# Moving the eviction and the store of the per-layer embedding's units to other engines

## The chip, the cores and the metric

The kernel runs on one core of one Trainium2 chip. The metric is device microseconds of one execution, as the median of several runs; lower is better.

## The reference: what is computed

One layer of a streaming encoder on 1024 prompt tokens and 8 samples of 16 new tokens, each sample with 1024 cached frames, in float32.

```python
xn = rms_norm(x, norm_g)
u, g_pool, c_q, c_kv, k_r, g_mla = jnp.split(xn @ w_in, SPLIT_IDX, axis=-1)
pool_out = multiscale_pool(...) * silu(g_pool)
attn = chunk_causal_attention(q_nope, q_rope, k_nope, krope_all, v, q_pos, k_pos)
h = x + concat([pool_out, attn * silu(g_mla)]) @ w_out
gate = sigmoid(rms_norm(h, ple_norm_g) @ w_ple_gate + b_ple_gate)
y = h + gate * (p @ w_ple)
```

The change is about the product `p @ w_ple` of the last line: `p` has 256 columns for each of the 1152 tokens, and `w_ple` is 256 x 2048. It hangs on nothing else, so it can be computed at any time before the last stage.

## The kernel before

Arrays lie transposed: 128 channels on the partitions, tokens along the free axis, in NT = 3 blocks of TB = 384 tokens. Every matrix product is made of three matmuls (`mm3`, lines 77 to 79): each operand is split into a rounded high half and a low half, and high x high, low x high and high x low are summed. A split (`split`, lines 68 and 69) is a copy by ScalarE, which makes the high half, and a subtraction, by VectorE or GpSimd, which makes the low one. So what TensorE multiplies has always passed ScalarE and then one of the others.

The stages follow one another: input projections and the pooling branch (to about 805 us of the profile), key and query projections of the attention (`phase2`, to about 985 us), attention of the samples over their caches (`attend_samples`, to about 1297 us), attention of the prompt (`attend_prompt`, to about 1670 us), output projection and gate (`phase5`).

The class `Embed` makes `p @ w_ple`. `block(t, cts)` handles one token block: it loads the two row tiles of `p` (line 782, tensor `pT`) and splits them into `h` and `l`, and then makes sixteen units, one for each group `ct` of 128 output channels. A unit loads its weights (`wraw`, line 786, 128 KB, ScalarE's DMA queue), splits them into `wh` and `wl` (two buffers each), makes six matmuls into one PSUM bank (`p`, one buffer; in the last block two units of three use a bank `k` of the sample attention instead), evicts the bank into a tile `ev` (line 794) and stores it to the scratch `ple` in device memory (line 795, 192 KB). The last stage reads `ple` again, more than 600 us later.

The 48 units are filler. Block 0 and half of block 1 are traced beside `phase2`, the other half of block 1 in the first sample (`between`), block 2 in the last weighing of the samples (`fill` in `attend_samples`; there, `issue_after(sh.last.ins)` holds its matmuls behind the last matmul of the sample scores). Behind them come the value projection of the samples (`ph`, `wvh`, lines 1429 to 1446) and the scores `s` of head 0 of the prompt attention, in whose gaps matmuls `f` of the output projection run (`out_units`, lines 1093 to 1121; weights `wraw` from `w_out`, moving tiles `M0h`, `M0l` from `mixp`). The prompt's heads are loaded by `load` (lines 1144 to 1166): tiles `qh`, `kh`, `stk`, `vh`, whose low halves GpSimd makes.

The order on each engine is not written out by hand. The tile framework schedules the traced instructions with a timing model of its own, and each engine then executes its list strictly in order, waiting where an input or a buffer is not there. A DMA is issued in order too, by the engine on whose queue it stands, and an engine that waits to issue one executes nothing behind it. So an edit of one line can move instructions anywhere.

Of the kernel before, what the change touches and what calls it, by code (L numbers as in the profile page):

```python
# [8 lines left out]
AF = mybir.ActivationFunctionType  # L9
# [10 lines left out]
P = 128  # L20
KT = D // P
TB = 384
# [742 lines left out]
class Embed:  # L765
# [8 lines left out]
    def block(self, t, cts=range(KT), bank=None):  # L774
        k, nc, io, pl = self.k, self.k.nc, self.k.io, self.pl
        if t != self.at:
            self.at = t
            self.ph = k.t(pl, [P, 2, TB], "h", F32R)
            self.pl_ = k.t(pl, [P, 2, TB], "l", F32R)
            for c in range(2):  # L780
                raw = k.t(pl, [P, TB], "raw")
                nc.scalar.dma_start(raw[:], io["pT"][t][:, c, :])
                k.split(self.ph[:, c, :], self.pl_[:, c, :], raw[:])
        for ct in cts:
            raw = k.t(pl, [P, 2, P], "wraw", bufs=4)
            nc.scalar.dma_start(raw[:], io["w_ple"][ct])
            wh = k.t(pl, [P, 2, P], "wh", F32R, bufs=self.bufs)
            wl = k.t(pl, [P, 2, P], "wl", F32R, bufs=self.bufs)
            k.split(wh[:], wl[:], raw[:])
            ps = bank() if bank and ct % 3 else k.t(self.pp, [P, 512], "p", bufs=self.banks)  # L790
            for c in range(2):
                k.mm3(ps[:, :TB], wh[:, c, :], wl[:, c, :], self.ph[:, c, :], self.pl_[:, c, :], c == 0, c == 1)
            ev = k.t(pl, [P, TB], "ev", bufs=2)
            nc.vector.tensor_copy(ev[:], ps[:, :TB])
            nc.scalar.dma_start(self.sc["ple"][t][:, ct, :], ev[:])


class Shared:
# [652 lines left out]
def phase5(k, sc, wp):  # L1451
# [16 lines left out]
    def fill(b, c, src):  # L1468
        raw = ev()
        nc.sync.dma_start(raw[:], src)  # L1470
        k.split(b[0][:, c, :], b[1][:, c, :], raw[:])

    mix = [block(mp, t, "M", KT // 2) for t in range(NT)]
    for t in range(NT):
        for c in range(KT // 2):
            fill(mix[t], c, sc["mixm"][t][:, c, :])
    yield
    pp = es.enter_context(tc.tile_pool(name="p6p", bufs=1, space=PSUM, reuse_waits="tile"))
    ap = es.enter_context(tc.tile_pool(name="p6a", bufs=1, side="right", reuse_waits="tile"))
    res = [block(ap, t, "A", KT) for t in range(NT - 1)]  # L1480
    acc = [k.t(ep, [P, TB], f"R{t}") for t in range(NT)]
    half = range(KT // 2, KT)
# [28 lines left out]
    w = w_gate(0)  # L1511
    lp = es.enter_context(tc.tile_pool(name="p6l", bufs=1, reuse_waits="tile"))
    res.append(block(lp, NT - 1, "A", KT))
    for c in range(KT):
        fill(res[-1], c, sc["h"][:, c, :])
# [164 lines left out]
```

## Time and profile before

| | us |
|---|---|
| median of 3 runs | 2307.72 |
| lowest and highest | 2302.0, 2310.47 |
| the profiled execution | 2295.69 |
| its span, first to last instruction | 2293.9 |
| TensorE busy in it | 2217.6 |
| VectorE, ScalarE, GpSimd busy | 1450.2, 985.4, 345.7 |

The profile speaks of engines as PE (TensorE; PEld is its weight load), DVE (VectorE), ACT (ScalarE), POOL (GpSimd) and SP (SyncE, which only issues DMAs). A q behind the name (ACTq) is the engine's sequencer. In rows of the timeline, the first two numbers are the start and the duration in us, then come engine, line and operation, output <- input, and in brackets how long the engine had been idle and what ended the wait. In rows of waits stand the total in us, how often, and the longest. In rows of groups stand the count, busy us and mean ns, and the idle time ahead.

### The profile page before, as it was taken

The numbers are of one execution on the slowest core, as the hardware profiler recorded it, in microseconds if no ns is written. First come the engines' busy times: TensorE is split into PE (matmuls) and PEld (weight loads), VectorE is DVE, ScalarE is ACT, GpSimd is POOL, SyncE is SP. The second block draws the span as 40 slices with busy tenths as digits, with TensorE's granted clock in tenths as the row PEclk, the third lists the DMA queues.
The fourth block names the chain that finished last, engine by engine and source line by source line (L and its number), as shares of the span: only waits on it lengthen the run. The fifth ranks groups of instructions, "written<-read, shape, count | busy, mean of one in ns | idle before, by whom it ended". The sixth has DMA issues, their size and how long they took to land.

```text
span 2293.9 us, 35989 instructions
## 1 busy us (share of the span) xinstructions
PE 2217.6 (97%) x12856; PEld 2160.4 (94%) x12856; DVE 1450.2 (63%) x3056; ACT 985.4 (43%) x2181; POOL 345.7 (15%) x317
## 2 busy tenths in 40 slices
PE   8989999999899999989999899999999999999999
PEld 7989999999899989979998799999999999999998
DVE  6787777776777668868887765555553345344343
ACT  6533335443333466756665543343342233232222
POOL 0000000001111000033552532221002221111110
PEclk9999999999999999999999799999999999999999
DMA  9574336556666766482222844443263333223221
GB/s 297 185 245 156 126 122 217 166 164 178 184 186 186 220 201 189 122 252 95 92 71 73 246 152 153 129 154 124 82 198 112 101 120 110 86 92 98 85 87 64
DMA packets 257299, 339.24 MB, mean 148 GB/s; under 512 B 45024, under 2 KB 207200, under 8 KB 257120
## 3 DMA queue, kind: packets, MB, share of 16 engines
q1 hardware_dynamic: 234240, 304.18, 42.9%
q10 hardware_dynamic: 19296, 23.21, 3.1%
q0 software_dynamic: 3584, 9.56, 1.7%
q8 instruction: 101, 1.65, 0.3%
q14 instruction: 78, 0.64, 0.1%
HBM read 235.74 MB, written 101.12 MB: 147 GB/s over the span
## 4 chain that ended last, share of the span: by engine, by line
PE 54%; DMA 7%; DVE 6%; issue 2%; ACT 2%; POOL 1%; SPq 0%; ACTq 0%; DVEq 0%; POOLq 0%
PE mm L77 8%; PE mm L79 8%; PE mm L78 8%; PE f L77 3%; PE f L79 3%; PE f L78 3%; PE k L78 2%; PE k L79 2%; PE k L77 2%; PE t L1213 1%; DMA rawcq<-cq 1%; PE o L79 1%; PE o L78 1%; PE s L78 1%; PE s L79 1%
## 5 line engine op out<-in xcount | busy, mean ns | idle before, releaser
L68 ACT ACTIVATE wh<-wraw 128x1024 fp32r<-128x1024 f32 (+3 forms) x237 | 182.2, 770 | 212.9 <-PE mm L177 125.7
L69 DVE TENSOR_TENSOR wl<-wraw,wh 128x1024 fp32r<-128x1024 f32 (+3 forms) x235 | 210.6, 897 | 69.9 <-ACT wh L68 67.3
L1536 DVE TENSOR_TENSOR ev<-mm,R 128x384 f32<-128x384 f32 x48 | 26.7, 557 | 174.2 <-PE mm L79 170.3
L1537 ACT ACTIVATE ev<-ev,gains 128x384 f32<-128x384 f32 x48 | 29.4, 612 | 224.5 <-DVE ev L1536 124.5
L71 ACT ACTIVATE wh<-wraw,gains 128x128 fp32r<-128x128 f32 x256 | 82.0, 391 | 52.5 <-ACT wh L71 31.6
L704 POOL DMA_DIRECT2D u<-u x24 | 13.1, 544 | 602.1 <-DVE frs3a L88 509.3
L1214 ACT ACTIVATE pth<-t 128x512 fp32r<-128x512 f32 (+2 forms) x96 | 46.3, 486 | 131.8 <-PE t L1213 130.8
L72 DVE SCALAR_TENSOR_TENSOR wl<-wraw,gains,wh 128x128 fp32r<-128x128 f32 x256 | 88.0, 390 | 17.5 <-ACT wh L71 16.4
L77 PE MATMUL k<-wkh,ch 128*128 128x448 f32 x256 | 95.2, 373 | 2.1 <-ACT ch L68 1.3
L78 PE MATMUL k<-wkh,cl 128*128 128x448 f32 x256 | 93.6, 365 | 0.6 <-DVE cl L69 0.6
L79 PE MATMUL k<-wkl,ch 128*128 128x448 f32 x256 | 93.7, 366 | 0.0
L79 PE MATMUL mm<-A2l,wh 128*128 128x384 f32 x256 | 86.0, 336 | 0.0
L77 PE MATMUL mm<-A2h,wh 128*128 128x384 f32 x256 | 86.0, 336 | 0.0
L78 PE MATMUL mm<-A2h,wl 128*128 128x384 f32 x256 | 86.0, 336 | 0.0
L77 PE MATMUL mm<-A0h,wh 128*128 128x384 f32 x256 | 85.8, 335 | 0.0
L79 PE MATMUL mm<-A0l,wh 128*128 128x384 f32 x256 | 85.7, 335 | 0.0
L78 PE MATMUL mm<-A1h,wl 128*128 128x384 f32 x256 | 85.7, 335 | 0.0
L78 PE MATMUL mm<-A0h,wl 128*128 128x384 f32 x256 | 85.7, 335 | 0.0
L79 PE MATMUL mm<-A1l,wh 128*128 128x384 f32 x256 | 85.5, 334 | 0.0
L77 PE MATMUL mm<-A1h,wh 128*128 128x384 f32 x256 | 85.5, 334 | 0.0
L1498 DVE TENSOR_TENSOR ev<-mm,ev 128x384 f32<-128x384 f32 x48 | 26.8, 558 | 86.3 <-PE mm L79 85.9
L1342 ACT ACTIVATE sq<-k 128x896 f32<-128x896 f32 x64 | 58.5, 914 | 51.7 <-PE k L1339 50.0
(803 smaller groups left out, 7822.6 us busy)
## 6 DMA issues: line engine op xcount, KB each, us to landing
wraw<-w_in SPq DMA_DIRECT2D x89, 512.0 KB, 4.6
part<-o SPq DMA_DIRECT2D x93, 192.0 KB, 2.7
q<-part SPq DMA_DIRECT2D x93, 192.0 KB, 3.4
wraw<-w_out SPq DMA_DIRECT2D x64, 256.0 KB, 3.4
wraw<-w_ple_gate SPq DMA_DIRECT2D x64, 256.0 KB, 3.2
ple<-ev ACTq DMA_DIRECT2D x48, 192.0 KB, 3.0
fev<-xT SPq DMA_DIRECT2D x48, 192.0 KB, 2.4
hp<-fev SPq DMA_DIRECT2D x48, 192.0 KB, 1.9
```

The source lines that it names most:

```text
L68: nc.scalar.activation(hi, src, AF.Copy)
L69: eng.tensor_tensor(lo, src, hi, ALU.subtract)
L71: nc.scalar.activation(hi, src, AF.Copy, scale=scale)
L72: eng.scalar_tensor_tensor(lo, src, scale, hi, ALU.mult, ALU.subtract)
L77: mm(out, sh, mh, start=start, stop=False)
L78: mm(out, sl, mh, start=False, stop=False)
L79: self.last = mm(out, sh, ml, start=False, stop=stop)
L1214: nc.scalar.activation(pth[:, :n, qq], tp[:, :n, :], AF.Copy)
L1342: nc.scalar.activation(sq[:].rearrange("p (g c) -> p g c", g=2), ps[:, :2, :KW], AF.Square)
L1498: nc.vector.tensor_tensor(h[:], ps[:, :TB], h[:], ALU.add)
L1536: nc.vector.tensor_tensor(g[:], ps[:, :TB], R[t][:], ALU.mult)
L1537: nc.scalar.activation(g[:], g[:], AF.Sigmoid, bias=k.b_ple_gate[:, ct:ct + 1])
```

## The change: what it does

```diff
@@ Embed.block
             for c in range(2):
-                raw = k.t(pl, [P, TB], "raw")
+                raw = k.t(pl, [P, TB], "ev", bufs=3)
                 nc.scalar.dma_start(raw[:], io["pT"][t][:, c, :])
                 k.split(self.ph[:, c, :], self.pl_[:, c, :], raw[:])
...
-            ev = k.t(pl, [P, TB], "ev", bufs=2)
-            nc.vector.tensor_copy(ev[:], ps[:, :TB])
-            nc.scalar.dma_start(self.sc["ple"][t][:, ct, :], ev[:])
+            ev = k.t(pl, [P, TB], "ev", bufs=3)
+            nc.scalar.activation(ev[:], ps[:, :TB], AF.Copy)
+            nc.gpsimd.dma_start(self.sc["ple"][t][:, ct, :], ev[:])
```

The eviction of a unit is made by ScalarE instead of VectorE. The store is issued from GpSimd's queue instead of ScalarE's. The raw tile of `p`, which had one buffer of its own, and the two buffers of `ev` become three buffers that both use. The room in on-chip memory stays the same. The scheduler then orders all engines anew: the first difference lies where block 0 begins, the last one in the last head of the prompt attention; what comes after is in the same order.

On ScalarE, at the beginning of block 2 (`ev` and `ple` are of the units, `wh_13701` is the weight of the second unit, `wh_13733` of the fourth, `wh_13749` of the fifth; `qh`, `kh` belong to head 0 of the prompt), before:

```order
L68 ACTIVATE wh_13701<-wraw_13699 128x256
L68 ACTIVATE wh_13717<-wraw_13715 128x256
L795 DMA ple_24_83<-ev_13680 128x384
L786 DMA wraw_13763<-w_ple 128x256
L795 DMA ple_24_83<-ev_13696 128x384
L68 ACTIVATE wh_13733<-wraw_13731 128x256
L786 DMA wraw_13779<-w_ple 128x256
L795 DMA ple_24_83<-ev_13712 128x384
L68 ACTIVATE wh_13749<-wraw_13747 128x256
```

and now:

```order
L794 ACTIVATE ev_13680<-p_13673 128x384
L68 ACTIVATE wh_13701<-wraw_13699 128x256
L794 ACTIVATE ev_13696<-k_13689 128x384
L68 ACTIVATE wh_13717<-wraw_13715 128x256
L786 DMA wraw_13763<-w_ple 128x256
L786 DMA wraw_13779<-w_ple 128x256
L794 ACTIVATE ev_13712<-k_13705 128x384
L68 ACTIVATE wh_13733<-wraw_13731 128x256
L68 ACTIVATE wh_13749<-wraw_13747 128x256
L794 ACTIVATE ev_13728<-p_13721 128x384
```

The stores have left the list. The evictions stand in it, and the cast of the fourth unit's weights now stands behind the eviction of the third, with the fifth's beside it.

On SyncE's queue, behind the loads for the prompt's heads (`qT`, `kT`, `qrT`, `v`) at the end of block 2 (`w_out` is for the output projection, `mixm` is the result of the value projection), before:

```order
L1151 DMA raw_14367<-v_102 128x512
L110 DMA wraw_14240<-w_out 128x512
L110 DMA wraw_14246<-w_out 128x512
L110 DMA wraw_14252<-w_out 128x512
L1151 DMA raw_14700<-qT_103 128x512
L1446 DMA mixm_18_77<-gate_13923 128x2x128
L1151 DMA raw_14706<-kT_101 128x512
L1161 DMA raw_14712<-qrT_104 64x512 x2
L110 DMA wraw_14258<-w_out 128x512
```

and now:

```order
L1151 DMA raw_14367<-v_102 128x512
L1446 DMA mixm_18_77<-gate_13923 128x2x128
L1151 DMA raw_14700<-qT_103 128x512
L1151 DMA raw_14706<-kT_101 128x512
L1446 DMA mixm_18_77<-gate_13923 128x2x128 x2
L1161 DMA raw_14712<-qrT_104 64x512 x2
L1151 DMA raw_14718<-v_102 128x512
L1446 DMA mixm_18_77<-gate_13923 128x2x128
L1177 DMA gate_14064<-gm_10_69 128x384
```

The loads of `w_out` come later: behind all four stores of the value projection and, further down, behind the first six loads of `mixp`. Their casts on ScalarE and their subtractions on VectorE moved with them, behind those of the value projection.

On TensorE, in head 0 of the prompt attention (`s` are scores of one block of queries, `t` the transposes of the softmax of an earlier block, `f` the output projection), before:

```order
L1213 MATMUL t_14159<-ident_134,e_14139 128x128 x2
L77 MATMUL f_14264<-M0h_14058,wh_14242 128x384
L78 MATMUL f_14264<-M0h_14058,wl_14243 128x384
L77 MATMUL s_14300<-kh_13560,qh_14101 128x512
L78 MATMUL s_14300<-kh_13560,ql_14102 128x512
L79 MATMUL s_14300<-kl_13561,qh_14101 128x512
```

and now:

```order
L1213 MATMUL t_14293<-ident_134,e_14220 128x128 x4
L77 MATMUL f_14264<-M0h_14058,wh_14242 128x384
L77 MATMUL s_14493<-kh_13560,qh_14101 128x512
L78 MATMUL s_14493<-kh_13560,ql_14102 128x512
L79 MATMUL s_14493<-kl_13561,qh_14101 128x512
```

The first `f` stood ahead of the fifth block's scores (`s_14300`); it now stands ahead of the seventh's (`s_14493`). On GpSimd, which had only the low halves in this place, the sixteen stores stand between them: four ahead of head 0's `ql` and `kl`, two behind these, and so on, one or two at a time.

## The prediction

> **What bounds the kernel now.** I read the page's first part, then a table of stages, and only then who waited for whom inside the stages in which units of `Embed` run.
>
> ```profile
> PE 2217.6 (97%) x12856; PEld 2160.4 (94%) x12856; DVE 1450.2 (63%) x3056; ACT 985.4 (43%) x2181; POOL 345.7 (15%) x317
> ```
>
> TensorE is busy for 97% of the 2293.9 us span, and the change adds and removes no matmul. So an edit on the other engines can be worth only what it puts into or takes out of TensorE's 76 us of idle time, and the time in which TensorE runs at a reduced clock. The table says where these are. Its columns are the stretch, its length, busy time of PE, PEld, DVE, ACT and POOL, the granted clock, the DMA share and GB/s.
>
> ```profile
> 800.00:985.00 185.00, 177.32 (x995) 164.81 (x994) 141.75 (x439) 129.23 (x446) 1.96 (x8) 0.97 0.57 172
> 985.00:1005.00 20.00, 13.03 (x67) 10.14 (x66) 16.45 (x44) 8.09 (x17) 0.44 (x1) 1.00 0.91 273
> 1005.00:1245.00 240.00, 238.52 (x1448) 225.95 (x1448) 199.19 (x372) 160.61 (x366) 112.12 (x68) 1.00 0.31 99
> 1245.00:1285.00 40.00, 30.86 (x156) 26.79 (x154) 27.95 (x65) 17.78 (x40) 17.86 (x15) 0.87 0.68 202
> 1285.00:1310.00 25.00, 20.78 (x95) 18.32 (x94) 14.71 (x38) 13.13 (x33) 7.86 (x7) 0.66 0.83 255
> 1310.00:1700.00 390.00, 386.24 (x2435) 372.79 (x2434) 228.04 (x483) 161.24 (x343) 75.76 (x61) 1.00 0.46 144
> ```
>
> I take length minus busy time times clock as what a stage loses. 985 to 1005 us loses 7.0 us. 1245 to 1310 us loses 40 - 30.86 x 0.87 = 13.2 and 25 - 20.78 x 0.66 = 11.3, together 24.5 us, of which 13.4 are idle and the rest half clock. 1005 to 1245 and 1310 to 1700 lose 1.5 and 3.8 us: there TensorE is full, and moving work between the others gives nothing. So the change is worth at most 7.0 + 24.5 = 31.5 us, in two places: the join between the projections and the sample attention (call it the join), and the end of the sample attention, where sixteen units run (the tail).
>
> In the tail, these are the waits of TensorE, of VectorE and of ScalarE:
>
> ```profile
> PE k L78 <- DVE wl L69: 5.4, 5, 2.1
> DVE ev L794 <- DMA ple<-ev: 5.9, 5, 2.0
> ACT wh L68 <- DMA wraw<-w_out: 2.7, 2, 2.5
> ```
>
> TensorE waits for the low half `wl` of a unit's weights, and VectorE waits for old stores to leave the two `ev` buffers. One unit shows how the second makes the first:
>
> ```profile
> 1253.87 0.33 PE L77 MATMUL k<-h,wh 128*128 128x384 f32 x1
> 1254.21 0.56 DVE L794 COPY ev<-p 128x384 f32<-128x384 f32 x1 [1.06 <-DMA ple<-ev]
> 1254.78 0.42 DVE L69 TENSOR_TENSOR wl<-wraw,wh 128x256 fp32r<-128x256 f32 x1
> 1255.26 0.45 PE L78 MATMUL k<-h,wl 128*128 128x384 f32 x1 [1.05 <-DVE wl L69]
> ```
>
> The eviction waits 1.06 us for a store. The next unit's `wl` stands behind it on VectorE, and TensorE, which had issued that unit's first matmul, sits 1.05 us.
>
> **The change part by part.** *The eviction* goes from VectorE to ScalarE.
>
> ```profile
> L794 DVE COPY ev<-p x38: 543/550/558, 827.3 to 1281.5; 128x384 f32<-128x384 f32 x38
> L930 ACT ACTIVATE qn<-pb x36: 470/492/530, 825.0 to 982.0; 128x384 f32<-128x384 f32 x36
> ```
>
> The second row is ScalarE on the same shape out of PSUM: 0.49 for 0.55 us. VectorE loses 48 x 0.55 = 26 us, ScalarE gains 48 x 0.49 = 24 us. From 800 to 985 us that is 16 units, 7.9 us onto ScalarE's 129 of 185: TensorE's matmuls of the projections cover it, so I cost it at nothing; if the cover went, it would be those 7.9 us.
>
> *The join.* Units there share one PSUM bank, so each unit's first matmul waits for the eviction before it. TensorE's waits from 800 to 1000 us for these first matmuls, and the shortest and the longest of them:
>
> ```profile
> PE p L77 <- DVE ev L794: 3.6, 5, 1.8
> PE p L77 <- DVE rsa L88: 0.8, 1, 0.8
> PE p L77 <- DVE rsa L89: 0.7, 1, 0.7
> ...
> 985.63 0.44 PE L77 MATMUL p<-h,wh 128*128 128x384 f32 x1 [0.21 <-DVE ev L794]
> 998.64 0.41 PE L77 MATMUL p<-h,wh 128*128 128x384 f32 x1 [1.80 <-DVE ev L794]
> ```
>
> Late evictions had other work ahead of them on VectorE, busy for 16.45 of these 20 us; ScalarE was busy for 8.09. The shortest wait, 0.21 us, is a hand-over without a queue. With 0.35 us on ScalarE, seven waits of 5.1 us become 2.5: -2.6 us, between 0 and -5.
>
> *The stores and the third buffer.* The store leaves ScalarE's queue (0.33 us of issue each) for GpSimd's. Before has the same 192 KB as loads on that queue, at 518 to 747 us:
>
> ```profile
> L795 ACTq DMA_DIRECT2D ple<-ev x48: 326/333/476, 827.8 to 1282.0; - x48
> DMA to landing us min/median/max: 1.9/3.0/7.3
> ...
> L710 POOL DMA_DIRECT2D ev<-gp x24: 536/538/544, 518.5 to 747.5; - x24
> DMA to landing us min/median/max: 2.6/4.5/7.2
> ```
>
> An issue takes 0.54 us of GpSimd and lands in 4.5 us instead of 3.0. A buffer is taken for 0.6 us (eviction and hand-over) plus the landing: before 3.6 over two buffers is one unit per 1.8 us, after 5.1 over three is one per 1.7 us. So by medians slower stores and the third buffer cancel, and the buffers don't set the pace. The ends are landings of 2.6 and 7.2 us: 1.07 and 2.6 us a unit. GpSimd's own work hides the issues: it was idle 16 us before its first split in the tail.
>
> ```profile
> 1263.13 1.43 POOL L69 TENSOR_TENSOR ql<-raw,qh 128x512 fp32r<-128x512 f32 x1 [16.24 <-ACT qh L68]
> ```
>
> The Trainium skill speaks against this part: the page "SBUF — State Buffer", section "SBUF: two separate sides", says that GpSimd can't write the descriptors of its DMAs while VectorE runs a copy that takes both port pairs; the section "A bandwidth-pool intuition that's wrong (but worth ruling out)" gives about 620 ns alone and 3100 ns beside it. By it a store would land some 2.5 us later, an estimate from that page, and a buffer would come free every 2.5 us. No row before shows a store from GpSimd; the loads' median of 4.5 against 3.0 us is in its direction, their maximum of 7.2 us against 7.3 is not.
>
> *The tail.* What a raw input shares with `ev` costs nothing: the last pair of `pT` loads is issued 200 us ahead of the tail.
>
> ```profile
> L782 ACTq DMA_DIRECT2D raw<-pT x6: 334/334/335, 805.4 to 1045.6; - x6
> ```
>
> What counts is how fast sixteen units run. Before, from the first to the last eviction:
>
> ```profile
> 1249.06 0.55 DVE L794 COPY ev<-p 128x384 f32<-128x384 f32 x1
> ...
> 1281.45 0.56 DVE L794 COPY ev<-p 128x384 f32<-128x384 f32 x1 [0.50 <-PE p L79]
> ```
>
> That is 32.4 us, 2.16 a unit. After, in ScalarE's order, casts of two units' weights follow one eviction, and then the next. A pair costs eviction 0.49, cast 0.42, split 0.42, the five matmuls left (about 1.0), four hand-overs of 0.1, and the partner unit's 1.05: 3.8 us, 1.9 a unit. ScalarE's own sum says the same: 16 evictions 7.9, 14 casts, the loads of three heads 12 x 0.63, nine of 0.5 for the last softmax and rotary keys, eight `ph`.
>
> ```profile
> L68 ACT ACTIVATE wh<-wraw 128x256 fp32r<-128x256 f32 x14 | 5.8, 415 | 13.3 <-PE k L79 2.7 <-DMA raw<-kT 2.3 <-DVE el L69 2.0
> L68 ACT ACTIVATE ph<-pv 128x256 fp32r<-128x256 f32 x8 | 3.2, 406 | 2.1 <-PE k L78 1.6 <-DVE pv L1394 0.4
> L1380 ACT ACTIVATE l<-l 128x384 f32<-128x384 f32 x3 | 1.5, 515 | 1.4 <-DVE l L1379 1.4
> L68 ACT ACTIVATE vh<-raw 128x512 fp32r<-128x512 f32 x3 | 1.9, 632 | 2.0 <-DVE mb L1372 1.0 <-DMA raw<-v 0.8 <-issue 0.2
> ```
>
> 7.9 + 5.8 + 7.6 + 4.5 + 3.2 = 29 us. ScalarE becomes the engine of the tail, and the units gain 32.4 - 29 = 3.4, I say -4 us.
>
> *What the new order moves.* The value projection (48 matmuls from `ph` and `pl`) took from the first to the last row here 14.7 us, because its `ph` stood on ScalarE behind casts that waited for `w_out`, as in the row between:
>
> ```profile
> 1282.91 0.33 PE L77 MATMUL k<-ph,wvh 128*128 128x128 f32 x1 [1.28 <-ACT ph L68]
> ...
> 1294.65 0.63 ACT L68 ACTIVATE wh<-wraw 128x512 fp32r<-128x512 f32 x1 [2.50 <-DMA wraw<-w_out]
> ...
> 1297.43 0.41 PE L79 MATMUL k<-pl,wvh 128*128 128x128 f32 x1
> ```
>
> In the new order no `w_out` load or cast stands there. Four rounds of two `ph`, two `pl`, and twelve matmuls at about 1.8 us are 7 us for 14.7; loads of `v` and `qrT` remain in between, so I take -5 (0 to -8). In return head 0 of the prompt attention has no output-projection matmuls until its seventh block of scores is next. Four softmax rounds (of the first four blocks) are then uncovered; before, with cover, the gaps in head 0 were
>
> ```profile
> 1304.40 0.44 PE L77 MATMUL f<-M0h,wh 128*128 128x384 f32 x1 [0.84 <-ACT M0h L68]
> 1317.87 0.45 PE L77 MATMUL f<-M1h,wh 128*128 128x384 f32 x1 [1.37 <-DVE fev L1116]
> 1327.81 0.41 PE L77 MATMUL f<-M2h,wh 128*128 128x384 f32 x1 [0.91 <-ACT e L1198]
> ```
>
> I add one such gap of some 0.8 us for each of the four rounds: +3 (0 to +6). From 1310 to 1700 us the order differs too, where only 3.8 us are idle: nothing to win, +1.5 to lose.
>
> **Sum:** -2.6 - 4 - 5 + 3 + 1.5 = -7.1 us on the profiled execution's 2295.69 us. That execution lies 12 us under the median of the runs shown, 2307.72 us (2302.0 to 2310.47). I take the difference to the median: 2307.7 - 7.1 = 2301 us. A measurement of this kernel can tell about 0.5%, 11.5 us, from no change.
>
> **The rivals.** *The tail collapses (faster).* VectorE is free of 16 evictions and of waits for stores, the last sample's softmax comes early, and TensorE never has the gap after which the clock halves (11 of the 24.5 us). What then stays is ScalarE's sum against TensorE's work, some 9 us of loss: -15 there, -4 at the join, +1 after: -18, 2290 us. For it: the waits of 5.4 and 5.9 us above. Against it: ScalarE keeps 29 us of work.
>
> *Stores from GpSimd land late (slower).* The wait for a buffer now stands on ScalarE, and with it the casts of later units, `ph`, and the heads' loads. Point of decision: (0.6 + landing) / 3 = 2.16, a landing of 5.9 us. At 7.2 us a unit takes 2.6: 16 x 0.44 = +7; the store also stands behind splits of 1.4 us on GpSimd; the value projection gains nothing, head 0 costs its 3, half clock lasts 3 us longer: +13, 2321 us. For it: the DMA share of 0.68 to 0.83 in the tail. Against it: the median of 4.5 us. By the skill's rule above, the landing would lie at this point or past it; the trace so far bears it out in part only.
>
> *Nothing moves.* The pace of a unit is the chain cast, split, matmul, not eviction or store, and what the units gain head 0 gives back: 0 to +3, 2309 us.
>
> **How the numbers follow.** Forecast (-13 to +1 us) 0.46, collapse 0.22, nothing 0.17, late stores 0.15. Past -11.5 us lie the collapse and a little of the forecast: faster 0.28. Past +11.5 us lies most of the late stores: slower 0.13. Same 0.59. The range takes in the collapse with some more (-24) and the late stores nearly whole (+11): 2284 to 2319 us; the forecast's own is 2294 to 2309.
>
> **What would show it.** In the join, TensorE's waits for `ev` no longer above 0.9 us, and 985 to 1005 us losing under 5. In the tail, evictions on ScalarE under 2.0 us apart; no wait of ScalarE for `ple<-ev`; landings of these stores near 4.5 us (5.9 or more: late stores). The value projection under 10 us. Head 0 with gaps of TensorE before its first `f`. Half clock for as long as before (mean 0.87 over 40 us and 0.66 over 25 make 27 us at 0.5) would refute the collapse. The forecast is wrong if 1245 to 1310 us loses more than 24.5 us, or if the prompt attention after it loses over 6 us more.

## The result, and the profile after

The changed kernel takes 2293.56 us (median of 7 runs, 2289.57 to 2298.2) against 2305.47 us for the kernel before (7 runs, 2302.0 to 2310.47) on the same chip: a ratio of 0.9947, 95% interval 0.9933 to 0.9961, or -12 us. Two later comparisons gave 0.994 (0.992 to 0.996) and 0.9969 (0.9951 to 0.9987). The forecast was 2301 us, range 2284 to 2319. The gain is half a percent: small, but the interval leaves out 1. One execution of e5 (2715 us) and one of e6 (8938 us), at granted clocks of 0.75 and 0.24, are left out of the ratios below.

The profiled execution after took 2295.59 us, span 2293.8, which is no shorter than the one shown of before. These are its rows for the engines, from the page, and for the same stretches (columns as in the prediction):

```profile
PE 2212.4 (96%) x12856; PEld 2157.2 (94%) x12856; DVE 1440.6 (63%) x3008; ACT 1000.8 (44%) x2229; POOL 371.7 (16%) x365
```

```profile
800.00:985.00 185.00, 176.54 (x998) 164.26 (x997) 136.65 (x424) 132.88 (x459) 10.59 (x24) 0.98 0.58 172
985.00:1005.00 20.00, 14.48 (x73) 11.39 (x71) 14.49 (x40) 12.31 (x31) 4.38 (x8) 0.95 0.83 263
1005.00:1245.00 240.00, 235.82 (x1416) 222.71 (x1415) 195.77 (x361) 159.61 (x365) 114.24 (x75) 1.00 0.32 103
1245.00:1285.00 40.00, 32.60 (x179) 29.00 (x177) 30.92 (x55) 25.69 (x62) 24.82 (x27) 0.91 0.57 173
1285.00:1310.00 25.00, 22.28 (x109) 20.33 (x109) 13.83 (x34) 13.36 (x35) 11.76 (x13) 0.73 0.72 225
1310.00:1700.00 390.00, 386.18 (x2437) 373.53 (x2436) 229.59 (x486) 162.26 (x345) 76.57 (x60) 1.00 0.47 149
```

By the same reckoning (length minus busy time times clock), the join loses 6.2 us where it lost 7.0, the end of the sample attention 10.3 + 8.7 = 19.0 where it lost 24.5, and the stretch before it 4.2 where it lost 1.5. That is too little to read 12 us from, and the two executions also reached the first matmul of the projections at different times (808.65 and 812.53 us), though the instructions ahead of it are the same, in the same order. So each kernel was profiled again, side by side on one chip. There the stages are read off TensorE's timeline by the first instruction of each. Before, second trace:

```profile
807.64 0.77 PE L77 MATMUL pb<-wkh,ckvh 128*128 128x512 f32 x1 [5.95 <-DVE o L529]
...
1003.42 1.11 PE L77 MATMUL k<-wkh,ch 128*128 128x448 f32 x2 [1.61 <-ACT ch L68]
...
1249.77 0.33 PE L77 MATMUL p<-h,wh 128*128 128x384 f32 x1
...
1285.89 0.33 PE L77 MATMUL k<-ph,wvh 128*128 128x128 f32 x1 [1.28 <-ACT ph L68]
...
1300.77 0.41 PE L77 MATMUL s<-kh,qh 128*128 128x128 f32 x1
...
1684.05 0.33 PE L77 MATMUL mm<-M0h,wh 128*128 128x384 f32 x1
```

and the change, second trace:

```profile
806.39 0.77 PE L77 MATMUL pb<-wkh,ckvh 128*128 128x512 f32 x1 [5.09 <-DVE o L529]
...
995.85 1.11 PE L77 MATMUL k<-wkh,ch 128*128 128x448 f32 x2 [3.06 <-ACT ch L68]
...
1243.42 0.34 PE L77 MATMUL p<-h,wh 128*128 128x384 f32 x1
...
1278.91 0.22 PE L77 MATMUL k<-ph,wvh 128*128 128x128 f32 x1
...
1288.33 0.41 PE L77 MATMUL s<-kh,qh 128*128 128x128 f32 x1
...
1672.33 0.33 PE L77 MATMUL mm<-M0h,wh 128*128 128x384 f32 x1
```

The differences of such rows, for all profiled executions of this study, in us (start: the first `pb`; then projections and join, up to the first sample scores; samples, up to the first unit of block 2; units, up to the value projection; value projection, up to the prompt's first score; prompt attention, up to the last stage; last stage, to the end of its last matmul; the sum without the start), and the ratio of the times to before with its 95% interval:

| kernel | start | proj. | samples | units | value | prompt | last | sum | ratio |
|---|---|---|---|---|---|---|---|---|---|
| before | 808.6 | 192.6 | 245.7 | 36.0 | 14.7 | 383.2 | 607.6 | 1479.8 | |
| before, again (e1) | 807.6 | 195.8 | 246.4 | 36.1 | 14.9 | 383.2 | 606.7 | 1483.1 | 0.9994 (0.9981 to 1.0006) |
| change | 812.5 | 190.3 | 246.7 | 38.2 | 10.3 | 382.6 | 607.7 | 1475.8 | 0.9947 (0.9933 to 0.9961) |
| change, again (e2) | 806.4 | 189.5 | 247.5 | 35.5 | 9.4 | 384.0 | 606.2 | 1472.1 | 0.994 (0.992 to 0.996) |
| change, third (e11) | 810.6 | 189.8 | 246.9 | 35.1 | 9.5 | 382.4 | 605.3 | 1469.0 | 0.9969 (0.9951 to 0.9987) |
| e3 eviction only | 810.7 | 195.2 | 248.0 | 34.7 | 10.5 | 388.8 | 607.0 | 1484.2 | 0.9998 (0.9986 to 1.001) |
| e4 store only | 807.8 | 193.6 | 249.3 | 41.5 | 12.0 | 387.7 | 607.1 | 1491.2 | 1.0008 (0.9994 to 1.0022) |
| e5 eviction, store | 808.4 | 191.2 | 252.9 | 42.6 | 11.0 | 386.7 | 609.0 | 1493.4 | 1.0031 (1.0018 to 1.0044) |
| e6 eviction, buffers | 810.4 | 192.6 | 246.8 | 30.3 | 12.3 | 390.0 | 606.9 | 1478.9 | 0.9972 (0.9957 to 0.9987) |
| e7 before, `w_out` later | 816.6 | 192.8 | 246.3 | 39.0 | 10.6 | 385.9 | 605.7 | 1480.3 | 0.999 (0.9975 to 1.0005) |
| e8 change, cache load early | 810.0 | 192.2 | 247.7 | 36.6 | 8.8 | 388.2 | 606.4 | 1479.9 | 0.9982 (0.9966 to 0.9998) |
| e9 e6, `w_out` held | 818.8 | 192.0 | 247.4 | 28.6 | 12.3 | 385.5 | 606.3 | 1472.1 | 0.9974 (0.9957 to 0.999) |
| e10 e3, `w_out` held | 813.6 | 196.8 | 247.7 | 34.5 | 10.2 | 382.7 | 607.4 | 1479.3 | 0.9977 (0.9963 to 0.9991) |
| e12 change, stores split, held | 821.0 | 190.0 | 247.9 | 33.7 | 11.5 | 386.4 | 606.3 | 1475.8 | 0.9964 (0.995 to 0.9977) |

Of two executions of before and three of the change, the means of the sum are 1481.4 and 1472.3: -9.1 us, in line with the -7 to -13 us between the medians of the times. It is made of -4.3 in the projections with the join, +1.0 in the samples, +0.2 in the units, -5.1 in the value projection, -0.2 in the prompt attention and -0.7 after it. The units of the change carry more: 26 small matmuls of the last weighing but one stand among them instead of in the samples, 3.0 us at full clock by their columns. So the columns must be kept in view where units are compared: 44598 in before, e1, e4 and e7; 51306 in the change (all traces), e5 and e8; 49002 in e12; 42678 in e3 and e10; 42294 in e6 and e9. A thousand columns are 0.45 us at full clock (0.173 us for 384, as the matmuls' starts show).

Most of the gain goes with less time of TensorE at half clock. These are the projections with the join, and then the units with the value projection, in the second trace of before and in the second of the change (columns as above; the third number from the end is the granted clock):

```profile
807.64:1003.42 195.78, 186.95 (x1025) 172.63 (x1025) 149.16 (x467) 132.77 (x453) 1.94 (x8) 0.95 0.57 171
1249.77:1300.77 51.00, 37.73 (x179) 31.80 (x178) 34.63 (x76) 23.32 (x52) 18.75 (x15) 0.83 0.72 219
```

```profile
806.39:995.85 189.46, 181.09 (x1025) 167.10 (x1025) 139.87 (x443) 139.58 (x476) 14.96 (x32) 0.99 0.58 174
1243.42:1288.33 44.91, 36.67 (x206) 32.70 (x204) 31.55 (x58) 27.59 (x65) 29.14 (x32) 0.89 0.65 201
```

Length times (1 - clock) is what a reduced clock takes away at most. The traces' stretches of half clock, added up, take 4.4 and 9.1 us of the projections in the two traces of before and 3.0, 2.6 and 1.4 in the three of the change; of the units with the value projection, 11.4 and 8.5, and 7.7, 5.1 and 3.7. Over all these stages that is 22.2 us before and 14.7 after, 7.5 of the 9.1. The times of all executions agree: in e2's comparison the mean clock is 0.9832 for before and 0.9878 for the change, which takes 38.7 and 27.8 us of their spans; in e11's, 36.1 and 31.3. What begins and ends these stretches was not tested.

### The profile page after: what moved, and what is told of

Same layout as the page of the kernel before. It is cut to its first block, busy times and chain, and to the rows that moved or that the text cites. A ratio compares the mean times of both kernels' runs of the same rounds, so it can differ in the third digit from the quotient of the medians.

```text
span 2293.8 us, 35988 instructions
## 1 busy us (share of the span) xinstructions
PE 2212.4 (96%) x12856; PEld 2157.2 (94%) x12856; DVE 1440.6 (63%) x3008; ACT 1000.8 (44%) x2229; POOL 371.7 (16%) x365
## 3 DMA queue, kind: packets, MB, share of 16 engines
q8 instruction: 101, 1.65, 0.3%
## 4 chain that ended last, share of the span: by engine, by line
PE 73%; DMA 12%; DVE 8%; ACT 3%; issue 3%; POOL 1%; SPq 1%; ACTq 0%; DVEq 0%; POOLq 0%
PE mm L77 8%; PE mm L79 8%; PE mm L78 8%; PE mm L176 7%; PE mm L175 7%; PE mm L177 7%; PE f L77 3%; PE f L79 3%; PE f L78 3%; PE k L79 2%; PE k L78 2%; PE k L77 2%; DMA u<-u 1%; DMA q<-part 1%; PE t L1213 1%
## 6 DMA issues: line engine op xcount, KB each, us to landing
part<-o SPq DMA_DIRECT2D x93, 192.0 KB, 2.8
q<-part SPq DMA_DIRECT2D x93, 192.0 KB, 3.5
ple<-ev POOLq DMA_DIRECT2D x48, 192.0 KB, 3.0
fev<-xT SPq DMA_DIRECT2D x48, 192.0 KB, 2.4
hp<-fev SPq DMA_DIRECT2D x48, 192.0 KB, 2.0
```

## The experiments

Each run has its edit as a diff against the kernel before, where nothing else is said. Two theories stood at the beginning. A: the evictions leave VectorE, and the join and the tail gain. C: the gain lies in the `w_out` loads that the scheduler moved out of the value projection. B in the first pair is that neither place gains.

**e1 and e2: both kernels again.** No edit.

> The kernel before, unchanged, for a second trace. The profiled execution shown of before lay 10 us under the median of its runs, so the two traces at hand do not show where the 12 us went. Theory A (the evictions leave VectorE: the join and the tail gain): this trace loses 7 us in the join and 24 to 30 us at the end of the sample attention, where the trace after lost 5.5 and 18; its time is 2298 to 2310. Rival B (the gain lies in stalls of transfers elsewhere, which the profiled execution before happened to lack): the join and the tail lose what they lost in the first trace, within 2 us, and 5 us or more of additional idle time of TensorE stand in stretches without units of the embedding.

> The changed kernel, unchanged, for a second trace and five more pairs of times. Ratio to before 0.993 to 0.997 (about -12 us) by both theories. Theory A: join loses 5 to 6 us, the stretch that answers to 1245 to 1310 us of before loses 16 to 20. Rival B: these differ from the first trace after by more than 4 us, or stand equal to those of before.

The rows above are theirs. The times of these two profiled executions are 2297.89 and 2285.73 us; of the 12.2 us, 1.2 lie ahead of the first `pb`, 6.3 in the projections and the join, 6.1 between the first unit of block 2 and the prompt's first score; the other stages together lose 1.4. Rival B falls: the gain is where units run. In the join the units' part is plain, here in the change:

```profile
981.94 0.44 PE L77 MATMUL p<-h,wh 128*128 128x384 f32 x1 [0.58 <-ACT ev L794]
983.84 0.44 PE L77 MATMUL p<-h,wh 128*128 128x384 f32 x1 [0.58 <-ACT ev L794]
987.66 0.44 PE L77 MATMUL p<-h,wh 128*128 128x384 f32 x1 [0.58 <-ACT ev L794]
991.47 0.44 PE L77 MATMUL p<-h,wh 128*128 128x384 f32 x1 [0.58 <-ACT ev L794]
```

Four of the seven hand-overs from ScalarE take 0.58 us and none takes longer, where the waits for VectorE were 0.21 to 1.82 in the second trace of before; all in all they fell from 4.9 to 3.0 us. But the first matmul of the scores then waits 3.06 us for `ch`, and waited 1.61 in the second trace of before: most of these 1.9 us is taken by what is late next.

**e3 and e4: one part alone.**

```diff
-            nc.vector.tensor_copy(ev[:], ps[:, :TB])
+            nc.scalar.activation(ev[:], ps[:, :TB], AF.Copy)
```

> Only the eviction goes to ScalarE; the store stays on ScalarE's queue, two buffers of ev, a buffer of its own for the raw inputs. Theory A: it has most of the gain, -8 to -14 us (ratio 0.994 to 0.9965); TensorE's waits in the join fall to 0.6 or less. In the tail the wait for the store (5.9 us of VectorE before) now stands on ScalarE. Rival C (the w_out loads moved behind the value projection make the gain, and not the evictions): here these loads stand in the middle of the value projection's stores, so no more than half of it, 0 to -6 us.

```diff
-            nc.scalar.dma_start(self.sc["ple"][t][:, ct, :], ev[:])
+            nc.gpsimd.dma_start(self.sc["ple"][t][:, ct, :], ev[:])
```

> Only the store goes to GpSimd's queue; VectorE evicts, two buffers. Theory A: 0 to -4 us (16 issues of 0.33 us less on ScalarE in the tail, the same waits of VectorE for stores, since a store lands in 3.0 us on either queue); the join's waits of up to 1.8 us stay. Rival C: half or more of the gain if the w_out loads leave the value projection; in this order they stand ahead of two of its stores, so 0 to -6.

Neither gains: 0.9998 and 1.0008. Theory A falls as it was put: e3 has none of the 8 to 14 us, and in its join the waits for evictions are up to 1.00 us. C had 0 to -6 us for both, so these two times don't decide it. By stages the eviction alone does gain 5.7 us from the units to the prompt (45.2 for 50.9 us), and gives as much back in the prompt attention (388.8 for 383.2). The store alone loses 3.3, 5.5 and 4.5 us in the samples, the units and the prompt, and gains 3 in the value projection. So the three parts don't add up, and two questions are left: what the buffers do, and what the prompt attention loses.

**e5 and e6: two parts of three.** e5 is the two diffs above together. e6 is the eviction with

```diff
-                raw = k.t(pl, [P, TB], "raw")
+                raw = k.t(pl, [P, TB], "ev", bufs=3)
...
-            ev = k.t(pl, [P, TB], "ev", bufs=2)
+            ev = k.t(pl, [P, TB], "ev", bufs=3)
```

> The change without its third part: eviction by ScalarE and stores on GpSimd's queue, but two buffers of ev, and the raw input with its own. By now two profiles of each kernel show the gain in two places: from the first matmul of the projections to the first of the sample scores (before 192.6 and 195.8 us, after 190.3 and 189.5), and from the first unit of block 2 to the first score of the prompt (50.7 and 51.0 against 48.5 and 44.9); and only the eviction, alone, has the second gain (45.1) but loses 5.6 us in the prompt attention, where ScalarE's casts of w_out wait for loads issued late and hold up the exponentials. Theory B (the buffers have a part: with two, ScalarE's evictions wait for old stores, 6.1 us where only the eviction was moved): ScalarE waits for stores again, 4 us or more in the tail, and the ratio is 0.997 to 1.000. Theory D (the buffers have none; the differences come from where the scheduler puts the casts and loads of w_out against the value projection and head 0): here the w_out loads stand among the value projection's stores and the first output projection behind the fifth block of scores, as in the eviction alone; then 386 to 390 us of prompt attention and the ratio is 0.997 to 1.000 without the waits for stores.

> The change without its second part: eviction by ScalarE into three shared buffers, stores stay on ScalarE's queue. Theory B: the third buffer takes away ScalarE's 6 us of waits for stores; the tail (first unit of block 2 to first score of the prompt) takes 43 to 45 us, ratio 0.994 to 0.997. Theory D: the w_out loads stand among the value projection's stores, the prompt attention takes 386 to 390 us instead of 383, which eats the tail's gain: ratio 0.998 to 1.001. A third (E: the stores' issues, 0.33 us each, cost ScalarE the tail): tail 48 or more.

Theory B is borne out in the waits for stores, and e5 is slower than it expected. These are ScalarE's waits for a buffer in the tail, and in e5 TensorE's for ScalarE; e3, e5 (two rows) and e6:

```profile
ACT ev L794 <- DMA ple<-ev: 6.1, 7, 1.8
```

```profile
ACT ev L794 <- DMA ple<-ev: 8.6, 6, 2.8
...
PE k L77 <- ACT ev L794: 5.2, 4, 3.4
```

```profile
ACT ev L794 <- DMA ple<-ev: 0.8, 1, 0.8
```

With two buffers, ScalarE waits 6.1 and 8.6 us for stores and keeps the later casts waiting behind it; with three, 0.8. With the same store and nearly the same columns, the units take 34.7 us with two buffers (e3) and 30.3 with three (e6); with the store on GpSimd's queue, 42.6 with two (e5) and 35.1 to 38.2 with three (the change). The change without the third buffer (e5) is slower than before, 1.0031. E falls (42.6 us for units and value projection in e6, where it had 48 or more). D has a part beside B: both lose in the prompt attention, 386.7 and 390.0 us. That the buffers have no part, as D also said, is refuted. e6's time, 0.9972, lies just outside the ranges of both, 0.994 to 0.997 and 0.998 to 1.001.

Where that is lost is seen when each matmul's start, from the prompt's first score on, is compared with the columns so far at full clock (0.173 us for 384). After 60000 columns, some 40 us in, before lags 8.9 and 9.0 us and the change 8.6, 10.8 and 9.2, but e3, e4, e5 and e6 lag 15.0, 12.0, 13.0 and 16.3. From there to the end of the stage each lags 24 to 27 us more. So it is head 0. In e6, ScalarE's timeline and then TensorE's:

```profile
1297.95 0.63 ACT L68 ACTIVATE wh<-wraw 128x512 fp32r<-128x512 f32 x1 [4.87 <-DMA wraw<-w_out]
1298.49 0.35 ACT L1198 ACTIVATE e<-s,m 128x128 f32<-128x128 f32 x1
```

```profile
1298.98 0.69 PE L77 MATMUL s<-kh,qh 128*128 128x384 f32 x1 [4.13 <-ACT e L1198]
...
1328.51 0.69 PE L77 MATMUL f<-M2h,wh 128*128 128x384 f32 x1 [4.52 <-DVE fev L1116]
```

A cast of `w_out` waits 4.87 us for its load, the first exponential stands behind it, and TensorE stands 4.13 us for that exponential. Half clock follows such stalls: in the first 50 us of the prompt attention the mean clock is 0.84 in e6 and 0.86 in e3, which takes 8 and 7 us, against 0.96 and 0.93 in before. ScalarE's waits for `w_out` in the first 35 us are 5.1, 6.0, 3.0 and 5.2 us in e3 to e6, and 0 to 0.4 in before and the change. Before issues these loads 13.5 us ahead of the prompt's first score; the change issues them 6 us behind it and casts them later still; e3 to e6 issue them in between.

**e7: before, with the `w_out` loads later.**

```diff
-        nc.sync.dma_start(sc["mixm"][NT - 1][:, 2 * g:2 * g + 2, TB - P:], gs)
+        k.vdone = nc.sync.dma_start(sc["mixm"][NT - 1][:, 2 * g:2 * g + 2, TB - P:], gs)
...
-        w = load_w(k, wp, io["w_out"][0], range(2), bufs=4)
+        with k.tc.issue_after(k.vdone.ins):
+            w = load_w(k, wp, io["w_out"][0], range(2), bufs=4)
```

> The kernel before, with one thing of the new order alone: the loads of the first output-projection weights are held behind the last store of the samples' value projection. Theory C (this move makes the gain): value projection 9 to 11 us instead of 14.6, nothing lost in head 0, ratio 0.994 to 0.997. Theory D: value projection 9 to 11, but the prompt attention loses 2 to 6 us since the output projection has to wait for its weights: ratio 0.998 to 1.001. The join stays as before (about 194 us) in both.

As D had it: the value projection falls from 14.8 to 10.6 us, and 2.7 us go in the prompt attention (ScalarE waits 3.0 us for `w_out` there); 0.999. What neither theory had: the units ahead take 39.0 us for 36.0, so the two stages together gain only 1.3. C, as the whole gain, falls. Up to the units TensorE's order in e7 is that of before, so its 192.8 us of projections are a third measurement of before's: one kernel's traces differ by 3 us in this stage.

**e8: the change, with the first cache load on another queue.** Against the change:

```diff
-        nc.sync.dma_start(raw[:], io["cache_T"][b][:, :, cols])
+        (nc.sync if b + f else nc.gpsimd).dma_start(raw[:], io["cache_T"][b][:, :, cols])
```

> The changed kernel, with the first sample's first cache load (512 KB) on GpSimd's queue instead of SyncE's. In the changed kernel the first matmul of the sample scores waits 2.4 and 3.1 us for the cast of this load, which SyncE issues 0.45 us after the last but one store of qT, at 995.3 and 987.6 us; in the eviction alone it waits 4.8. If the units no longer set the end of the join, but this load does: here the load is issued 2 us or more earlier, the wait falls under 1 us, and the kernel gains another 2 to 3 us on the change (ratio to before 0.9925 to 0.9945). If the load's memory comes free only then, or the units still set the end, it gains nothing (0.994 to 0.996).

The load is issued at 990.8 us, ahead of the store of `qT` instead of behind it, and gains nothing: the ratio, 0.9982, lies above both of the expected ranges, and the projections with the join take 192.2 us. In the rows of SyncE and ScalarE in this run, and of TensorE:

```profile
991.44 0.36 SPq L950 DMA_DIRECT2D qT<-T  x1
```

```profile
1001.10 1.06 ACT L68 ACTIVATE ch<-raw 128x1024 fp32r<-128x1024 f32 x1 [5.12 <-DMA qT<-T]
```

```profile
1002.21 1.12 PE L77 MATMUL k<-wkh,ch 128*128 128x448 f32 x2 [5.17 <-ACT ch L68]
```

The cast `ch` now waits for the store of `qT` to end, 9.7 us after its issue. That would fit if the cast writes to memory that the store still reads, which was not shown; the wait got longer, not shorter. In this order of instructions the prompt attention also takes 388.2 us, without a wait for `w_out`: TensorE stands 3.25 us there for the eviction `fev` of the output projection's only bank, as it stands 4.52 in e6. So the wait for `w_out` is one of two stalls in head 0, and the other is this eviction, which in e8 has subtractions and scalings of the next blocks ahead of it on VectorE.

**e9, e10 and e11: the hold.** The loads of the first `w_out` tiles are held on SyncE's queue behind the sixth load of `mixp`, where the change has them. e9 is e6 with this, e10 is e3 with this, and e11 is the change beside them.

```diff
-            nc.sync.dma_start(raw[:], sc["mixp"][t][:, c, :])
+            k.mdma.append(nc.sync.dma_start(raw[:], sc["mixp"][t][:, c, :]))
...
-        w = load_w(k, wp, io["w_out"][0], range(2), bufs=4)
+        with k.tc.issue_after(k.mdma[5].ins):
+            w = load_w(k, wp, io["w_out"][0], range(2), bufs=4)
```

> The eviction and the three buffers (as in the run before with stores on ScalarE's queue), and the loads of the first output-projection weights held on SyncE's queue behind the sixth load of mixp, which is where they stand in the change. So far, where ScalarE waits for w_out inside the first 35 us of the prompt attention (3.0 to 6.0 us in five runs), the first 60000 matmul columns there lose 12 to 16 us; where it doesn't (before and the change), 8.6 to 10.7. Theory D (that wait, with the exponentials behind it on ScalarE, is what ate the eviction's gain): no wait for w_out of 1 us or more there, prompt attention 382 to 385 us instead of 390, tail 42 to 45, ratio to before 0.9935 to 0.9955, as good as the change. Rival F (the prompt attention loses for another reason, such as an earlier arrival at data that is not there yet): 387 to 391 us again, ratio 0.996 to 0.998.

> The eviction alone, two buffers, with the same hold on the w_out loads. Theory D: prompt attention 382 to 386 us instead of 388.8, tail 45 as there, ratio 0.997 to 0.9985: the eviction alone is then worth 4 to 7 us, less than with the third buffer, since ScalarE still waits 6 us for stores. Rival F: 388 to 390 us, ratio 0.999 to 1.001.

> The changed kernel once more, for a comparison on the same chip with the two runs beside it, and for a third trace: ratio 0.993 to 0.996, from the projections' first matmul to the sample scores 189 to 191 us, tail 44 to 49, prompt attention 382 to 385.

No wait for `w_out` is left in head 0 of e9 and e10. The prompt attention falls from 390.0 to 385.5 and from 388.8 to 382.7 us. So the place of these loads makes 4.5 of the 6.8 us that e6 loses there and all that e3 loses, and rival F, with 387 us or more, is refuted. What is not shown is that the wait for `w_out` alone does it, as D had it: with the hold the stalls for `fev` shrink too (e3 to e10 from 4.1 to 1.2 us), and the runs don't part the two. In the first 50 us the mean clock is back at 0.94 (e9) and 0.96 (e10). The change itself (e11) came out as expected by stages, and at 0.9969 a little above the range set for it. e10's time is as D had it: the eviction alone is worth 0.9977 once head 0 doesn't pay for it. In e9 units and value projection take 40.9 us, ten less than in before with the same matmuls, and the sum is that of the change (1472.1); but the time, 0.9974, is less than D expected and no better than the change beside it (0.9969). Its start, 818.8 us, is late, see the last section. Head 0 of e9, on TensorE:

```profile
1306.78 0.50 PE L77 MATMUL s<-kh,qh 128*128 128x512 f32 x1 [1.20 <-ACT e L1201]
...
1314.73 0.44 PE L78 MATMUL f<-M0h,wl 128*128 128x384 f32 x1 [1.16 <-DVE wl L69]
...
1332.13 0.41 PE L77 MATMUL f<-M2h,wh 128*128 128x384 f32 x1 [1.52 <-DVE fev L1119]
```

Both stalls of e6 have shrunk, from 4.13 and 4.52 to 1.20 and 1.52, and a small third has come.

**e12: an attempt at better.** Against the change, with e9's hold:

```diff
-            nc.gpsimd.dma_start(self.sc["ple"][t][:, ct, :], ev[:])
+            (nc.scalar if t == 2 else nc.gpsimd).dma_start(self.sc["ple"][t][:, ct, :], ev[:])
```

> An attempt at a version better than the change: the change, with the stores of block 2 (the tail) back on ScalarE's queue and the w_out loads held behind the sixth load of mixp. In three traces of the change, from the first unit of block 2 to the value projection's start it takes 35.1 to 38.2 us with 26 matmuls of the last but one weighing among the units (3.0 us at full rate); with eviction and buffers, stores on ScalarE's queue, 30.3 and 28.6 without them. Theory G (the store's place on GpSimd's queue is what slows the units of the tail): 32 to 34 us here, prompt attention 382 to 386, and 2 to 4 us better than the change: ratio to before 0.992 to 0.995. Rival H (it is the order of the weighing's matmuls, which is the same here as in the change): 35 to 38 us again, ratio 0.995 to 0.998, no better than the change.

The units take 33.7 us, in G's range. But six of their matmuls (2304 columns, 1.0 us) stand in the value projection here, and both stages together take 45.2 us, where the change has 48.5, 44.9 and 44.6 for the same matmuls. So the place of the stores gains nothing that these traces show. Of the distance from the change's shortest 35.1 us to e9's 28.6, 4.1 us are 9012 columns that e9 has elsewhere; the rest is not settled. The prompt attention takes 386.4 us (3.42 us of it for `fev`), and at 0.9964, in H's range, it beats nothing. No kernel of this study was better than the change.

## Why the prediction was right or wrong

The time lay in the range, 7 us under the forecast. The predicted sum was -7.1 us on the profiled execution, and the traces' means give -9.1; but this closeness is in part luck. Terms of both signs failed, and the clock, which makes up to 7.5 of the 9.1, has no term in the sum: the prediction had it in the rival of the collapse alone.

- **The join**, -2.6: the waits for the unit before fell from 4.9 us (six rows of the first trace of before) to 3.0 (seven rows of the first trace after), none over 0.6; over all of 800 to 1000 us, from 5.1 to 3.6, where 2.5 was predicted, since a hand-over took up to 0.58 us and not 0.35. The step that was missing is what comes next: the first scores' wait for `ch` grew from 1.30 and 1.61 us to 2.36, 3.06 and 2.95, so that by waits the join gained under 1 us, and by the lag against the columns 1 to 2, by where the cut is made. 985 to 1005 us lost 6.2, where under 5 was said. The stage gained 4.3: 2 to 3 us lie ahead of the join, where I had costed the edit at nothing. About 885 us TensorE stood 1.18 and 0.93 us in before, and 0.56 and 0.89 in the change's second trace. From 875 to 895 us the mean clock was 0.91 and 0.74 in the two traces of before, which takes 1.8 and 5.2 us, and 1.00 in all three of the change. So half clock is enough for the part ahead of the join; why the inputs came earlier there was not tested, and with e7 in mind the size is uncertain by some 3 us.
- **The buffers**: "by medians slower stores and the third buffer cancel" was wrong twice. A store from GpSimd's queue isn't slower:

```profile
L795 POOL DMA_DIRECT2D ple<-ev x48: 539/539/602, 828.8 to 1296.6; - x48
...
DMA to landing us min/median/max: 2.1/3.0/7.0
```

  The landing is 3.0 us, as on ScalarE's queue, not 4.5: the loads were no stand-in for stores. The issue took 0.54 us, as taken. And the third buffer isn't cancelled by anything: with two, the eviction on ScalarE waits 6 to 9 us, and the change would have been slower than before (e5). The late-stores rival fell with the landing. By the Trainium skill, page "SBUF — State Buffer", the section "A bandwidth-pool intuition that's wrong (but worth ruling out)", the landing should have been some 2.5 us longer beside a copy of VectorE, an estimate from that page's figures; these 48 stores don't show it. They are no hard test, though: the page speaks of a copy that takes both port pairs, and of VectorE's 49 copies while they ran, 41 read PSUM and eight (`mb`) another tile. The issue of a store overlaps these eight for 0.15 us at most. In e4, where VectorE evicts from PSUM beside such stores, the median landing is 3.1 us.
- **The units**, -4: wrong by about 4. The step that failed is "ScalarE becomes the engine of the tail", with its 29 us of work taken for the pace. The three traces of the change give 35.1 to 38.2 us for the units, with 3.0 us of moved matmuls in them. From first to last eviction, which is how the prediction measured its 32.4 us, they take 38.0 to 42.0 (2.5 us and more each, under 2.0 was said). What TensorE waits for in the tail is VectorE, as before: 8.2, 8.1 and 8.7 us in the change's three traces, 8.5 and 8.7 in those of before (stretches of 49 to 55 us about it), and for ScalarE 1.3, 0 and 0.3 us, where it was 3.8 and 4.3. In the first trace after, the low halves of the units' weights still lead:

```profile
PE p L78 <- DVE wl L69: 2.7, 2, 1.9
PE k L78 <- DVE wl L69: 1.5, 3, 0.7
```

  e9's 28.6 us are not the same work: 4.1 us of the change's columns stand elsewhere there. Whether the order of the weighing among the units keeps the change from less is not settled (e12).
- **The value projection**, -5: measured -5.1. The reason given (no `w_out` load or cast in it) is shown in part only: e7 makes this move alone and has -4.2 in this stage, but starts it 3.0 us later. e3, with these loads still among its stores, has 10.5 us too. And most of the 5.1 is clock: half clock took 6.3 and 6.8 us of this stage in before (mean clock 0.57 and 0.54) and 3.5, 1.7 and 2.0 in the change (0.67, 0.82 and 0.79). The term's size came out right, its working, by rounds of 1.8 us, in small part only.
- **Head 0**, +3, **and the order after it**, +1.5: measured -0.2 together. The step that failed is "one such gap of some 0.8 us for each of the four rounds". TensorE's gaps up to the first `f` of the change:

```profile
1304.97 0.50 PE L77 MATMUL s<-kh,qh 128*128 128x512 f32 x1 [0.64 <-ACT e L1198]
```

  There is one, of 0.64 us, and none longer in its other two traces. What costs there in the other orders is not the missing cover. In e3 to e7 it goes with casts of output-projection weights that stand on ScalarE ahead of the exponentials while their loads are out; the change has them late enough. In e8 and e12 it goes with the wait for `fev`. And a stall costs more than its length: of the 6.8 us that e6 loses in this stage, half clock makes up to 5.
- **The collapse**: half clock from 1245 to 1310 us is 20.7 us (0.91 over 40 us, 0.73 over 25, at 0.5) after 27: shorter, so not refuted outright, and not away. The rival was nearer to what happened than its 0.22 says: in the units with the value projection the time lost to half clock fell by 4.5 us, nearly all of what these two stages gained. No wait of ScalarE for stores in the tail was rightly said for the change.

## What to carry to other kernels

Where a scheduler orders all engines, an edit of four lines is priced twice: for what it does, and for where everything else lands. Profile the parts alone and together, cut each trace at the first instructions of the stages, and compare stage by stage: e3 and e6 held a gain of 6 to 8 us in one stage that another gave back, and a hold on one load gave 4.5 and 6.1 us in that stage. Read the granted clock of each stage beside its length: here a stall is paid twice, as idle time and as the half clock behind it, and most of the gain goes with the second. When an in-order engine takes over an eviction, count its buffers first, since a wait for a buffer there stops all that stands behind it.

## What was not expected of the hardware

Three subtractions of VectorE, 0.55 us each where GpSimd does nothing, took 4.22 us while GpSimd made subtractions (VectorE and GpSimd in the change's first trace; the second trace has 4.21):

```profile
1267.57 4.22 DVE L69 TENSOR_TENSOR el<-l,eh 128x384 fp32r<-128x384 f32 x3 [0.53 <-ACT eh L68]
```

```profile
1267.25 1.29 POOL L69 TENSOR_TENSOR vl<-raw,vh 128x512 fp32r<-128x512 f32 x1 [0.82 <-POOL stk L1164]
1268.49 1.33 POOL L69 TENSOR_TENSOR krl<-raw,krh 128x384 fp32r<-128x384 f32 x1
```

The Trainium skill, in the page "SBUF — State Buffer", section "Who interferes with whom", says that a VectorE instruction with two inputs in SBUF contends with a GpSimd instruction that reads SBUF. The rows agree in direction, with 2.6 times the time for the three. It is no single case: in the first trace of before, too, three subtractions of this form took 1.65 us each, with GpSimd at work for 1.24 us of it.

And a stage that the change doesn't touch is no constant: the first matmul of the projections came at 806.4 to 821.0 us in the fourteen traces, with the same order of instructions ahead of it. So a single pair of profiles can hide a gain of 10 us, as the first pair here did. The four kernels with a hold on a load (e7, e9, e10, e12) began at 813.6 to 821.0, all others at 806.4 to 812.5. With one trace of each, and no edit ahead of that point, what makes this stays open.
